# Private buffers for the expert stage, a recurrence in head pairs, a shorter candidate list: one NeuronCore kernel for two transformer blocks

## The chip, the cores and the metric

The kernel is one program on one core of a Trainium2 chip. TensorE (PE) multiplies matrices, VectorE (DVE) and ScalarE (ACT) work on elements, GpSimd (POOL) issues the gathers, SyncE (SP) issues every other transfer. The metric is device time of one execution in microseconds (us): the median of the runs shown.

## The reference

Two blocks follow each other on x of 512 tokens by 1024 columns, all in float32. Cut to what the change touches:

```python
# block 1, four heads of a gated delta rule, 8 chunks of 64 tokens, one after the other
def step(state, inp):
    u_i, w_i, qd_i, kd_i, a_i, gl_i = inp
    v_new = u_i - w_i @ state
    o_i = qd_i @ state + a_i @ v_new
    state = state * gl_i[..., None, None] + jnp.swapaxes(kd_i, -1, -2) @ v_new
    return state, o_i
# beside it, four heads of sparse attention: out = g0 * o_c + g1 * o_s + g2 * o_w
# block 2 ends with product-key experts (8 heads, 128 * 128 experts), 128 tokens at a time
v1, i1 = lax.top_k(s1, 16); v2, i2 = lax.top_k(s2, 16)
cand = (v1[..., :, None] + v2[..., None, :]).reshape(128, 8, -1)      # 256 sums
top_s, pos = lax.top_k(cand, 16)
experts = jnp.take_along_axis(cand_idx, pos, axis=-1)
gate = softmax(top_s)
act = gelu(einsum('chkd,cd->chk', u[experts], hc))
out = einsum('chk,chkd->cd', gate * act, v[experts])
```

## The kernel before

Activations lie transposed, features on the 128 partitions and tokens along the row. A float32 product is made of three fast ones: `split` (lines 192 to 194) writes the high part of a tile by a cast on ACT and the low part by a subtraction on DVE, and `mm3` or `gemm` adds high*high, high*low and low*high in PSUM. The order of instructions on every engine is fixed when the program is built: a list scheduler takes the code in program order as priority and moves work past what waits, as far as buffers allow. So the engines' queues are static, and an instruction that waits holds up all that stands behind it on its engine.

Block 1, the stretch around the change (lines 475 to 484). `proj_qv` makes the projections of one head (three-product GEMMs with 512 columns), `gdn_fin` finishes its chunk matrices, `nsa(t)` does the attention of 128 query tokens for four heads: scores (tiles ks, kw), softmax on DVE and ACT, transposes (L902), products with the values (pt, vn). `gdn_scan` walks the 8 chunks of the recurrence with all four heads side by side: first products w,T (called V here), a subtraction (L753), products w,kN (S), scaling and addition of the state (L759, L760), output products qA,w and at,w (O), a copy (L765). V and O write PSUM bank 0 and S writes bank 1, one tile each, so the next V waits for the copy of this O.

Block 2, `peer`. For 384 of the 512 tokens all 16384 experts are computed densely in 128 blocks of 128 experts, and a gate tensor picks out the selected ones; the last 128 tokens gather the rows of their experts one selected slot at a time. Three parts overlap: `route` finds the 16 best pairs per head and token group (lines 1203 to 1283), `spread` builds the gates by one-hot products (tiles o, L1294 to L1304) and writes them to DRAM, except the last 32 tokens, which stay in glast. Beside both, `run_ahead` does the expert-key GEMM of a block (row, rowhi, rowlo; 24 matmuls) and spills its 128x384 result, 113 to DRAM and 15 kept on chip. The last stage (lines 1120 to 1161) then does for each of the 128 blocks e: load the spilled result (pact) and, for four blocks at once, the gates (gtile); multiply by gtile and by glast (L1139, L1140); split into pwh and pwl; load the expert-value rows into a row buffer and split them into vh and vl; 24 matmuls into eight PSUM banks. `gather_sum` gathers one row of the last 128 tokens' experts per block (L1174, POOL) and adds it into pN on DVE (L1191). Expert-key rows, expert-value rows and these gathered rows share one ring of six row buffers; pact has four buffers, vh, vl, pwh and pwl four.

Of the kernel before, what the change touches and what calls it, by code (L numbers as in the profile page):

```python
# [9 lines left out]
F32 = mybir.dt.float32  # L10
F32R = mybir.dt.float32r
# [4 lines left out]
ALU = mybir.AluOpType  # L16
# [4 lines left out]
P = 128  # L21
S = 512
D = 1024
# [7 lines left out]
ND = 384  # L31
# [119 lines left out]
class Builder:  # L151
# [248 lines left out]
    def block1(self):  # L400
        A, V, x = self.A, self.V, self.x
        with ExitStack() as st1:
# [55 lines left out]
            with ExitStack() as st2:  # L458
                self.gi = self.pool(st2, "gi")
                self.pj = self.pool(st2, "pj")  # L460
                with ExitStack() as nst:
                    self.nk = self.pool(nst, "nk")
                    self.gdn_gates()
                    self.banks(2, 3)
                    for h in range(4):
                        self.proj_k(h, hi, lo, started[h][0] if h < len(started) else None)
                        self.gdn_inv(h)
                    self.banks()
                    self.proj_kv(hi, lo)
                    self.nsa_keys(self.nk)  # L470
                self.mod_queue(0, (2, 4, 3))
                self.proj_nq(hi, lo)
                kp = self.pool(st2, "nt")
                self.nsa_begin(kp)
                for h in range(4):
                    self.proj_qv(h, hi, lo)
                    self.gdn_fin(h)
                    if h < 2:
                        self.nsa(kp, h, False)
                self.gdn_scan()  # L480
                for h in range(4):
                    if h % 2:
                        self.nsa(kp, 2 + h // 2, True)
                    self.proj_gz(h, hi, lo)
            hst.close()
            op = self.pool(st1, "op", side="right")
            mh = self.mh = op.tile([P, KD, S], F32R, name="mh")
# [232 lines left out]
    def gdn_fin(self, h):  # L720
        V, C = self.V, self.C
        r4 = lambda v: v.rearrange("p a b -> p (a b)")
        q, k, vN, E, X = self.qT[h], self.kT[h], self.vN[h], self.at[h], self.X[h]
        psq = self.ps(0)
# [7 lines left out]
        ps = self.ps(0)  # L732
# [5 lines left out]
    def gdn_scan(self):  # L738
        V, C, gi = self.V, self.C, self.gi
        wT, at, qd, kd = self.wT, self.at, self.qd, self.kd  # L740
        St = gi.tile([P, 4, P], F32, name="w0", bufs=2)
        V.memset(St, 0.0)
        oT = self.eq
        for c in range(8):
            t, o = divmod(c * 64, P)
            r = slice(o, o + 64)
            tb = slice(t * P, (t + 1) * P)
            cs = slice(c * 64, c * 64 + 64)
            psv = self.ps(0)
            for h in range(4):  # L750
                self.mm(psv[:, h * P:(h + 1) * P], wT[h][:, tb], St[:, h, :])
            vnew = gi.tile([P, 4, P], F32, name="w1", bufs=2)
            V.tensor_tensor(vnew[r], self.kA[r, :, tb], psv[r].rearrange("p (h d) -> p h d", h=4), ALU.subtract)  # L753
            if c < 7:
                psS = self.ps(1)
                for h in range(4):
                    self.mm(psS[:, h * P:(h + 1) * P], kd[h][r, t, :], vnew[r, h, :])
                Sn = gi.tile([P, 4, P], F32, name="w0", bufs=2)
                V.tensor_tensor(Sn, St, self.gl[:, c, :].unsqueeze(2).to_broadcast([P, 4, P]), ALU.mult)  # L759
                V.tensor_tensor(Sn, Sn, psS.rearrange("p (h d) -> p h d", h=4), ALU.add)  # L760
            pso = self.ps(0)
            for h in range(4):
                self.mm(pso[:, h * P:h * P + 64], St[:, h, :], qd[h][:, cs], True, False)
                self.mm(pso[:, h * P:h * P + 64], vnew[r, h, :], at[h][r, t, o:o + 64], False, True)
            C.copy(oT[:, :, cs], pso.rearrange("p (h b) -> p h b", h=4)[:, :, 0:64])  # L765
            if c < 7:
                St = Sn
        self.oT = oT

    def gdn_out(self):  # L770
        V, C, G, gp, oT = self.V, self.C, self.G, self.gp, self.oT
# [285 lines left out]
    def peer(self):  # L1057
        A, V, C, x = self.A, self.V, self.C, self.x
# [3 lines left out]
        with ExitStack() as st:  # L1062
# [57 lines left out]
            with ExitStack() as st2:  # L1120
                wk = self.pool(st2, "pe")
                bank = [self.ps(m) if m < 6 else self.acc() for m in range(KD)]
                self.sqp = (wk, 4)
                part = []
                for e in range(P):
                    if e == 0 or e % GA == 2:
                        n, e0 = min(GA, P - e) if e else 2, e
                        if e:
                            gt = wk.tile([P, NB - 1, GA, TB], F32, name="gtile", bufs=2)[:, :, :n, :]
                        else:  # L1130
                            gt = self.hN[:, :(NB - 1) * n * TB].rearrange("p (b a t) -> p b a t", b=NB - 1, a=n)
                        self.dma(gt, gd[:, :, e:e + n, :].rearrange("b p a t -> p b a t"))
                    if e < KEPT:
                        act = ra.tile([P, ND], F32, name="pact", bufs=4)
                        self.dma(act, sp[e])
                    else:
                        act = kept[e]
                    a3 = act.rearrange("p (b t) -> p b t", t=TB)
                    V.tensor_tensor(a3[:, :NB - 1, :], a3[:, :NB - 1, :], gt[:, :, e - e0, :], ALU.mult)  # L1139
                    V.tensor_tensor(a3[:, NB - 1, :], a3[:, NB - 1, :], gl[:, e, :], ALU.mult)  # L1140
                    wh = wk.tile([P, ND], F32R, name="pwh", bufs=LAST + 1)
                    wl = wk.tile([P, ND], F32R, name="pwl", bufs=LAST + 1)
                    self.split(wh, wl, act)
# [59 lines left out]
    def route(self, rp, hi, lo, T3, run_ahead):  # L1203
# [7 lines left out]
        self.gi = self.gs_ = 0  # L1211
        qlane = self.lane(rp, "wqr", 2, 2)
        qbank = self.bank_ring(0, 1, acc=0)


        def chosen(px, ix, n, out=None):
# [3 lines left out]
            V.tensor_scalar(ab[:, 0], px, 4, None, ALU.logical_shift_right)  # L1220
            V.tensor_scalar(ab[:, 1], px, 15, None, ALU.bitwise_and)
# [15 lines left out]
        for h in range(8):  # L1237
            first = self.gemms([A["wq"][s] for s in range(2)], hi, lo, lane=qlane, bank=qbank) if h == 0 else None
            for s in range(2):
# [7 lines left out]
                C.copy(sc.rearrange("p a b -> p (a b)"), ps)  # L1247
                for t in (3, 0, 1, 2):
                    self.top16(sc[:, t, :], v_[:, t, h, s, :], ix[:, t, h, s, :])
            for t in (3, 0, 1, 2):  # L1250
                cand = rp.tile([P, 16, 16], F32, name="cand", bufs=2)
                b3 = [P, 16, 16]
                V.tensor_tensor(cand, v_[:, t, h, 0, :].unsqueeze(2).to_broadcast(b3),
                                v_[:, t, h, 1, :].unsqueeze(1).to_broadcast(b3), ALU.add)
                self.top16(cand.rearrange("p a b -> p (a b)"), ts[:, t, h, :], px[:, t, h, :])
# [87 lines left out]
```

## Time and profile before

| | us |
|---|---|
| median of 3 runs | 2481.82 (2474.93 to 2487.04) |
| the profiled execution | 2477.21 |
| its span | 2475.1 |
| PE, DVE, ACT, POOL busy | 2378.9 (96%), 1843.3 (74%), 1077.1 (44%), 337.5 (14%) |

A busy PE is not a PE at its full pace, since records overlap; the pace is the number of matmuls in a stretch (the x behind a busy time). The stages in us from the start of the span: recurrence and attention, 288 to 406; routing with run-ahead GEMMs, 1120 to 1620; gates with run-ahead GEMMs, to 1879; the last stage, to 2458.

### The profile page before, as it was taken

Reading aid. Unit: us, or ns where it says so; the run is one execution under the profiler, and the core shown is the slowest. Engines: PE = TensorE matmul, PEld = TensorE weight load, DVE = VectorE, ACT = ScalarE, POOL = GpSimd, SP = SyncE. Lnnn points to the kernel's source line nnn. Section 1 sums busy time; section 2 is a strip of 40 time slices with the busy share of each in tenths; the row PEclk is TensorE's granted clock in tenths of the full one; section 3 lists DMA queues with packets and bytes.
Section 4 is the critical chain, followed back from the end, with each engine's and each line's share of the span. In section 5 each row is a group of like instructions: output and inputs, shape, how many; then the busy total and the mean of one; then the engine's idle time right before and its main releaser. Section 6 shows DMA issues by size and latency. Waiting matters only on the chain.

```text
span 2475.1 us, 35106 instructions
## 1 busy us (share of the span) xinstructions
PE 2378.9 (96%) x12749; PEld 2150.7 (87%) x12749; DVE 1843.3 (74%) x3826; ACT 1077.1 (44%) x1753; POOL 337.5 (14%) x284
## 2 busy tenths in 40 slices
PE   7999999899999999998999999999998999899998
PEld 7788787678878777877899999999998999899997
DVE  6774635788874389665999999899876777787764
ACT  4534624343332233334323334499995333333332
POOL 0000000000000000000232331233101222223310
PEclk9999989899999999998999999999998999999999
DMA  7341102566554222225478897689867999899981
GB/s 276 125 133 60 52 9 85 170 198 193 188 183 144 81 90 92 70 86 188 148 239 291 319 369 259 202 320 345 321 228 244 301 312 311 301 330 327 325 266 52
DMA packets 197934, 509.40 MB, mean 206 GB/s; under 512 B 20352, under 2 KB 93312, under 8 KB 195840
## 3 DMA queue, kind: packets, MB, share of 16 engines
q1 hardware_dynamic: 160896, 372.92, 44.4%
q0 software_dynamic: 36864, 134.23, 15.3%
q8 instruction: 100, 1.64, 0.3%
q14 instruction: 74, 0.61, 0.1%
HBM read 459.71 MB, written 47.38 MB: 205 GB/s over the span
## 4 chain that ended last, share of the span: by engine, by line
PE 58%; DVE 13%; DMA 13%; issue 7%; ACT 6%; POOL 2%; POOLq 0%; DVEq 0%; SPq 0%; ACTq 0%
PE p L162 38%; PE acc L162 19%; DMA row<-in_ev_dram,eidx 7%; DMA raw<-in_ada_dram 2%; ACT o L1296 1%; POOL row L1174 1%; ACT gstage L1304 1%; DVE grow L1181 1%; DVE pN L1191 1%; DVE wlo L194 1%; DMA araw<-in_ada_dram 1%; DVE vl L194 1%; DMA pact<-spill 1%; ACT rowhi L193 1%; DVE rowlo L194 1%
## 5 line engine op out<-in xcount | busy, mean ns | idle before, releaser
L193 ACT CAST whi<-raw 128x1024 fp32r<-128x1024 f32 (+2 forms) x152 | 150.7, 993 | 386.7 <-PE p L162 239.1
L162 PE MATMUL p<-pwl,vh 128*128 128x384 f32 x768 | 262.7, 342 | 25.0 <-DVE pwl L194 24.5
L162 PE MATMUL p<-pwh,vh 128*128 128x384 f32 x768 | 258.3, 338 | 5.2 <-ACT pwh L193 5.2
L162 PE MATMUL p<-pwh,vl 128*128 128x384 f32 x768 | 259.2, 338 | 0.0
L194 DVE TENSOR_TENSOR wlo<-raw,whi 128x1024 fp32r<-128x1024 f32 (+2 forms) x152 | 174.8, 1151 | 102.9 <-ACT whi L193 100.5
L193 ACT CAST vh<-row 128x1024 fp32r<-128x1024 f32 x128 | 134.3, 1051 | 257.3 <-PE acc L162 186.1
L1174 POOL DMA_INDIRECT row<-in_ev_dram,eidx x128 | 161.1, 1259 | 501.5 <-DVE pN L1191 188.4
L1191 DVE SCALAR_TENSOR_TENSOR pN<-row,dots,pN 128x1024 f32<-128x1024 f32 x127 | 162.7, 1281 | 84.9 <-DMA row<-in_ev_dram,eidx 84.6
L193 ACT CAST rowhi<-row 128x1024 fp32r<-128x1024 f32 x128 | 134.5, 1051 | 206.4 <-PE acc L162 94.6
L194 DVE TENSOR_TENSOR rowlo<-row,rowhi 128x1024 fp32r<-128x1024 f32 x128 | 155.8, 1218 | 35.6 <-ACT rowhi L193 35.5
L162 PE MATMUL p<-hi,rowhi 128*128 128x384 f32 x512 | 174.6, 342 | 3.2 <-ACT hi L301 2.6
L162 PE MATMUL p<-lo,rowhi 128*128 128x384 f32 x512 | 175.5, 343 | 1.8 <-DVE lo L302 1.8
L162 PEld LDWEIGHTS p<-pwl,vh 128*128 128x128 f32 x768 | 146.0, 190 | 35.8 <-DVE pwl L194 35.6
L162 PE MATMUL acc<-lo,rowhi 128*128 128x384 f32 x512 | 175.2, 342 | 0.0
L162 PE MATMUL acc<-hi,rowlo 128*128 128x384 f32 x512 | 174.8, 342 | 0.3 <-DVE rowlo L194 0.3
L162 PE MATMUL acc<-hi,rowhi 128*128 128x384 f32 x512 | 174.5, 341 | 0.6 <-ACT rowhi L193 0.6
L162 PE MATMUL p<-hi,rowlo 128*128 128x384 f32 x512 | 174.9, 342 | 0.1
L194 DVE TENSOR_TENSOR vl<-row,vh 128x1024 fp32r<-128x1024 f32 x128 | 155.9, 1219 | 24.7 <-ACT vh L193 24.7
L162 PE MATMUL p<-hi,whi 128*128 128x512 f32 x416 | 164.8, 402 | 5.7 <-ACT hi L301 4.3
L162 PE MATMUL p<-hi,wlo 128*128 128x512 f32 x416 | 166.8, 401 | 1.1 <-DVE wlo L194 1.0
L162 PE MATMUL p<-lo,whi 128*128 128x512 f32 x416 | 165.6, 399 | 0.9 <-DVE lo L302 0.9
L162 PEld LDWEIGHTS p<-pwh,vh 128*128 128x128 f32 x768 | 145.8, 190 | 5.6 <-ACT pwh L193 5.5
(525 smaller groups left out, 6055.0 us busy)
## 6 DMA issues: line engine op xcount, KB each, us to landing
row<-in_eu_dram SPq DMA_DIRECT2D x128, 512.0 KB
row<-in_ev_dram SPq DMA_DIRECT2D x128, 512.0 KB
araw<-in_ada_dram SPq DMA_DIRECT2D x64, 512.0 KB
raw<-in_up_dram SPq DMA_DIRECT2D x44, 512.0 KB
gdram<-gstage SPq DMA_DIRECT2D x11, 2048.0 KB
gtile<-gdram SPq DMA_DIRECT2D x31, 704.0 KB
spill<-pact SPq DMA_DIRECT2D x113, 192.0 KB
pact<-spill SPq DMA_DIRECT2D x113, 192.0 KB
```

What stands on the lines that cost most here:

```text
L162: self.T.matmul(out, lhsT, rhs, start=start, stop=stop)
L193: self.C.copy(hi, src)
L194: self.V.tensor_tensor(lo, src, hi.bitcast(F32), ALU.subtract)
L1174: self.G.indirect_dma_start(out=u, out_offset=None, in_=self.A[src], in_offset=bass.IndirectOffsetOnAxis(ap=self.eidx[:, s:s + 1], axis=0))
L1181: self.V.scalar_tensor_tensor(u, u, 1.0, self.hN, ALU.mult, ALU.mult, accum_out=self.dots[:, s:s + 1])
L1191: self.V.scalar_tensor_tensor(self.pN, v, w, self.pN, ALU.mult, ALU.add)
L1296: C.activation(o2[:, i, :], self.iota, AF.Abs, bias=T3[:, 1, t:t + 1])
L1304: C.copy(gs[:, :, q * 4:q * 4 + 4].rearrange("p a t -> p t a"), ps.rearrange("p (t a) -> p t a", t=4))
```

## The change

Four edits. (1) The projections run in two head pairs, and the recurrence runs once per pair after its projections; each chunk does two heads, and V, S and O of a chunk share bank 0. The attention of all four token groups stands behind both recurrences, beside the last projections. (2) Of the 256 sums of two sorted lists of 16 only 112 are formed: the first 4 of the one with all 16 of the other, the other 12 with the first 4; `chosen` maps positions in the shorter list back. (3) In the last stage the expert-value rows keep the six row buffers, the gathered rows get six of their own (grow), the spilled results six of their own (vact), and vh, vl use the three high and low pairs of the run-ahead GEMMs and one new pair, in turn. (4) The gates of the last 32 tokens are copied beside the loaded ones on ACT, four blocks at once, so that one multiplication per block does.

```diff
-                for h in range(4):
-                    self.proj_qv(h, hi, lo)
-                    self.gdn_fin(h)
-                    if h < 2:
-                        self.nsa(kp, h, False)
-                self.gdn_scan()
+                for pair in ((0, 1), (2, 3)):
+                    for h in pair:
+                        self.proj_qv(h, hi, lo)
+                        self.gdn_fin(h)
+                    self.gdn_scan(pair)
                 for h in range(4):
-                    if h % 2:
-                        self.nsa(kp, 2 + h // 2, True)
                     self.proj_gz(h, hi, lo)
+                    self.nsa(kp, h, h > 1)
...
+            ps = self.ps(0)
+            psv, psS = half(ps, 0), half(ps, 1)
+            for i, h in enumerate(pair):
+                self.mm(psv[:, i * P:(i + 1) * P], wT[h][:, tb], St[:, i, :])
...
+                pair = lambda: [wk.tile([P, D], F32R, name=n, bufs=1) for n in ("vh", "vl")]
+                vring = ulane[1] * LAST + [pair]
+                self.row = lambda: wk.tile([P, D], F32, name="grow", bufs=6)
...
-                        self.dma(gt, gd[:, :, e:e + n, :].rearrange("b p a t -> p b a t"))
+                        self.dma(gt[:, :NB - 1], gd[:, :, e:e + n, :].rearrange("b p a t -> p b a t"))
+                        C.copy(gt[:, NB - 1], gl[:, e:e + n, :])
                     if e < KEPT:
-                        act = ra.tile([P, ND], F32, name="pact", bufs=4)
+                        act = wk.tile([P, ND], F32, name="vact", bufs=6)
...
-                    V.tensor_tensor(a3[:, :NB - 1, :], a3[:, :NB - 1, :], gt[:, :, e - e0, :], ALU.mult)
-                    V.tensor_tensor(a3[:, NB - 1, :], a3[:, NB - 1, :], gl[:, e, :], ALU.mult)
+                    V.tensor_tensor(a3, a3, gt[:, :, e - e0, :], ALU.mult)
...
-                    vh = wk.tile([P, D], F32R, name="vh", bufs=LAST + 1)
-                    vl = wk.tile([P, D], F32R, name="vl", bufs=LAST + 1)
+                    vring.append(vring.pop(0))
+                    vh, vl = vring[-1]()
...
+            V.tensor_scalar(wide, px, 124, None, ALU.bitwise_and)
+            V.tensor_scalar(wide, wide, 64, 3, ALU.max, ALU.mult)
+            V.scalar_tensor_tensor(wide, wide, 192, px, ALU.subtract, ALU.add)
...
+                for i0, i1, nj in ((0, 4, 16), (4, 16, 4)):
...
+                    V.tensor_tensor(o, a, b, ALU.add)
```

How the queues move, first on PE in the recurrence: a chunk of before, with V (w, T) for four heads, attention products (pc, pt, pr) and S (w, kN).

```order
L878 MATMUL p_2774<-ca,sc 32x128 x4
L162 MATMUL p_2583<-w_2570,T_575 128x128
L162 MATMUL p_2583<-w_2570,T_743 128x128
L162 MATMUL p_2583<-w_2570,T_942 128x128
L162 MATMUL p_2583<-w_2570,T_1141 128x128
L162 MATMUL p_2798<-pc,vcn 128x128
L162 MATMUL p_2798<-pt,vn 128x128 x3
L902 MATMUL p_2811<-ca,pr 128x128 x3
L162 MATMUL p_2838<-pc,vcn 128x128
L162 MATMUL p_2590<-w_2588,kN 128x128 x4
```

The same engine now, at the first of the chunks that stand among attention products:

```order
L162 MATMUL acc<-kw,x 128x384
L162 MATMUL p_2052<-w_2044,T_575 128x128
L162 MATMUL p_2052<-w_2044,T_743 128x128
L162 MATMUL p_2052<-w_2055,kN 128x128 x2
L878 MATMUL p_2494<-ca,sc 32x128 x4
L162 MATMUL p_2052<-qA,w_2044 128x64
L162 MATMUL p_2052<-at,w_2055 128x64
```

A chunk now has two heads, and there are 16. The V of three of them stand among the projection GEMMs, those of thirteen behind them. The stretch behind the projections held 79 GEMM matmuls before and holds 37 now.

Second, ACT at the entry of the last stage, before (glast: the copies of the last gates; vh: the first expert-value rows):

```order
L1296 ACTIVATE o_16285<-ca,T_8309 128x128 x3
L1297 ACTIVATE o_16262<-o_16262 128x384
L1304 COPY glast<-p_16248 128x4x128
L1297 ACTIVATE o_16285<-o_16285 128x384
L1304 COPY glast<-p_16268 128x4x128
L1304 COPY glast<-p_16291 128x4x128
L193 CAST vh<-row 128x1024 x4
L193 CAST pwh<-pact 128x384 x4
```

and now (kept: the result of a run-ahead GEMM; rowhi: here the first three expert-value rows):

```order
L1322 COPY glast<-p_16325 128x4x128
L193 CAST rowhi<-row 128x1024
L1101 ACTIVATE kept_16426<-p_16395 128x384
L1322 COPY glast<-p_16348 128x4x128
L1136 COPY hN<-glast 128x64
L193 CAST rowhi<-row 128x1024
L1101 ACTIVATE kept_16459<-p_16428 128x384
L193 CAST rowhi<-row 128x1024
L1101 ACTIVATE kept_16492<-acc 128x384
L193 CAST rowhi<-row 128x1024
L1101 ACTIVATE kept_16525<-acc 128x384
```

Three run-ahead results are now stored behind the last gate copy, none before; on PE 71 run-ahead matmuls stand behind the last one-hot product, where there were none and the last 20 one-hot products (five rows of four) stood in one run.

Third, DVE in the body of the last stage, two blocks of before and two of now:

```order
L194 TENSOR_TENSOR vl<-row,vh 128x1024
L1139 TENSOR_TENSOR pact<-pact,gtile 128x352
L1140 TENSOR_TENSOR pact<-pact,glast 128x32
L194 TENSOR_TENSOR pwl<-pact,pwh 128x384
L1191 SCALAR_TENSOR_TENSOR pN<-row,dots,pN 128x1024
```

```order
L194 TENSOR_TENSOR rowlo<-row,rowhi 128x1024
L194 TENSOR_TENSOR pwl<-vact,pwh 128x384
L1143 TENSOR_TENSOR vact<-vact,gtile 128x384
L1194 SCALAR_TENSOR_TENSOR pN<-grow,dots,pN 128x1024
L194 TENSOR_TENSOR vl<-row,vh 128x1024
```

The sum into pN keeps its place in the queue; the row that it reads now comes from its own ring.

## Rows read from the trace of the kernel before

**Rows 1.** Windows: busy us (instructions) of PE, PEld, DVE, ACT, POOL; PE clock; DMA share; GB/s.
```profile
288.00:406.00 118.00, 114.32 (x581) 90.36 (x580) 49.56 (x137) 39.62 (x98) 0.00 (x0) 0.84 0.06 20
...
1310.00:1560.00 250.00, 248.78 (x1422) 248.07 (x1421) 244.47 (x621) 94.89 (x132) 65.34 (x60) 1.00 0.84 302
...
1869.00:1894.00 25.00, 15.81 (x72) 14.63 (x72) 14.51 (x45) 16.01 (x28) 5.47 (x3) 0.73 0.68 211
1894.00:2160.00 266.00, 249.27 (x1391) 241.68 (x1390) 193.49 (x287) 88.55 (x117) 61.79 (x56) 0.99 0.88 301
2180.00:2260.00 80.00, 80.00 (x464) 80.00 (x463) 63.25 (x95) 28.51 (x38) 23.64 (x19) 1.00 0.94 331
2260.00:2400.00 140.00, 132.71 (x753) 129.93 (x752) 107.73 (x162) 47.49 (x63) 42.74 (x25) 1.00 0.91 311
```
**Rows 2.** Waits in the last stage, 1894 to 2400: us in total, times, longest.
```profile
POOL row L1174 <- DVE vl L194: 157.8, 42, 9.3
...
DVE pN L1191 <- DMA row<-in_ev_dram,eidx: 76.1, 50, 5.7
DVE pact L1139 <- DMA pact<-spill: 48.3, 39, 2.9
...
PE p L162 <- DVE pwl L194: 23.6, 24, 2.4
```
**Rows 3.** Instruction groups, 1894 to 2400: busy us, mean ns, idle before them.
```profile
L194 DVE TENSOR_TENSOR vl<-row,vh 128x1024 fp32r<-128x1024 f32 x113 | 137.7, 1218 | 0.0
L1191 DVE SCALAR_TENSOR_TENSOR pN<-row,dots,pN 128x1024 f32<-128x1024 f32 x106 | 135.9, 1282 | 76.3 <-DMA row<-in_ev_dram,eidx 76.1
...
L194 DVE TENSOR_TENSOR pwl<-pact,pwh 128x384 fp32r<-128x384 f32 x109 | 60.1, 551 | 0.0
L1139 DVE TENSOR_TENSOR pact<-pact,gtile 128x352 f32<-128x352 f32 x109 | 56.9, 522 | 48.5 <-DMA pact<-spill 48.3
...
L1140 DVE TENSOR_TENSOR pact<-pact,glast 128x32 f32<-128x32 f32 x109 | 20.3, 186 | 0.0
```
**Rows 4.** Issues of transfers, 1900 to 2400: kind, count, KB each.
```profile
row<-in_ev_dram SPq DMA_DIRECT2D x113, 512.0 KB
pact<-spill SPq DMA_DIRECT2D x105, 192.0 KB
gtile<-gdram SPq DMA_DIRECT2D x28, 704.0 KB
```
**Rows 5.** PE at the entry of the last stage: start, us, work [idle before].
```profile
1869.17 1.95 PE L162 MATMUL p<-o,o 128*128 128x128 f32 x16
...
1883.87 2.29 PE L162 MATMUL p<-pwh,vh 128*128 128x384 f32 x6 [5.19 <-ACT pwh L193]
...
1888.55 0.52 PE L162 MATMUL p<-pwl,vh 128*128 128x384 f32 x1
1888.87 0.52 PE L162 MATMUL p<-pwh,vl 128*128 128x384 f32 x1
```
**Rows 6.** ACT there.
```profile
1879.53 3.88 ACT L193 CAST vh<-row 128x1024 fp32r<-128x1024 f32 x4
```
**Rows 7.** PE groups of the recurrence, 288 to 406.
```profile
L162 PE MATMUL p<-at,w 64*128 64x64 f32 x64 | 15.7, 330 | 0.0
L162 PE MATMUL p<-qA,w 128*128 128x64 f32 x64 | 15.3, 324 | 0.1
...
L162 PE MATMUL p<-w,T 128*128 128x128 f32 x64 | 10.3, 314 | 0.0
...
L162 PE MATMUL p<-w,kN 64*128 64x128 f32 x56 | 9.0, 307 | 0.8 <-DVE w L753 0.8
```
**Rows 8.** One window inside that stretch, columns as in rows 1.
```profile
320.00:340.00 20.00, 20.00 (x80) 16.60 (x80) 3.67 (x9) 4.24 (x11) 0.00 (x0) 0.57 0.00 1
```
**Rows 9.** DVE groups of the routing, 1180 to 1545.
```profile
L1198 DVE MATCH_REPLACE8 rsc<-tv,rsc 128x128 f32<-128x128 f32 x56 | 15.6, 289 | 0.0
...
L1198 DVE MATCH_REPLACE8 cand<-ts,cand 128x256 f32<-128x256 f32 x32 | 13.2, 413 | 0.0
```

More of the change, by code (lines that the diff above doesn't have):

```diff
@@ L723, in gdn_fin @@
         q, k, vN, E, X = self.qT[h], self.kT[h], self.vN[h], self.at[h], self.X[h]
-        psq = self.ps(0)
+        psq = self.ps(4)
         for t in range(TT):
@@ L731, in gdn_fin @@
         V.tensor_tensor(vN, vN, self.rn[:, h, :].unsqueeze(2).to_broadcast([P, TT, P]), ALU.mult)
-        ps = self.ps(0)
+        ps = self.ps(4)
         for t in range(TT):
@@ L735, in gdn_fin, with gdn_scan @@
         C.copy(k, ps)
-    def gdn_scan(self):
+    def gdn_scan(self, pair):
         V, C, gi = self.V, self.C, self.gi
         wT, at, qd, kd = self.wT, self.at, self.qd, self.kd
-        St = gi.tile([P, 4, P], F32, name="w0", bufs=2)
+        h0 = pair[0]
+        hs = slice(h0, h0 + 2)
+        new = lambda k: gi.tile([P, 4, P], F32, name=f"w{k}", bufs=2)[:, 0:2, :]
+        St = new(0)
         V.memset(St, 0.0)
-        oT = self.eq
+        oT = self.oT = self.eq
+        half = lambda ps, i: ps[:, i * 2 * P:(i + 1) * 2 * P]
         for c in range(8):
@@ L748, in gdn_scan @@
             cs = slice(c * 64, c * 64 + 64)
[L749 to L753, printed above, removed]
-            if c < 7:
[L755 to L765, printed above, removed]
+            ps = self.ps(0)
+            psv, psS = half(ps, 0), half(ps, 1)
+            for i, h in enumerate(pair):
+                self.mm(psv[:, i * P:(i + 1) * P], wT[h][:, tb], St[:, i, :])
+            vnew = new(1)
+            V.tensor_tensor(vnew[r], self.kA[r, hs, tb], psv[r].rearrange("p (h d) -> p h d", h=2), ALU.subtract)
+            if c < 7:
+                for i, h in enumerate(pair):
+                    self.mm(psS[:, i * P:(i + 1) * P], kd[h][r, t, :], vnew[r, i, :])
+                Sn = new(0)
+                V.tensor_tensor(Sn, St, self.gl[:, c, hs].unsqueeze(2).to_broadcast([P, 2, P]), ALU.mult)
+                V.tensor_tensor(Sn, Sn, psS.rearrange("p (h d) -> p h d", h=2), ALU.add)
+            for i, h in enumerate(pair):
+                self.mm(psv[:, i * P:i * P + 64], St[:, i, :], qd[h][:, cs], True, False)
+                self.mm(psv[:, i * P:i * P + 64], vnew[r, i, :], at[h][r, t, o:o + 64], False, True)
+            C.copy(oT[:, hs, cs], psv.rearrange("p (h b) -> p h b", h=2)[:, :, 0:64])
             if c < 7:
                 St = Sn
-        self.oT = oT
     def gdn_out(self):
@@ L1128, in peer @@
                         if e:
-                            gt = wk.tile([P, NB - 1, GA, TB], F32, name="gtile", bufs=2)[:, :, :n, :]
+                            gt = wk.tile([P, NB, GA, TB], F32, name="gtile", bufs=2)[:, :, :n, :]
                         else:
-                            gt = self.hN[:, :(NB - 1) * n * TB].rearrange("p (b a t) -> p b a t", b=NB - 1, a=n)
-                        self.dma(gt, gd[:, :, e:e + n, :].rearrange("b p a t -> p b a t"))
+                            gt = self.hN[:, :NB * n * TB].rearrange("p (b a t) -> p b a t", b=NB, a=n)
+                        self.dma(gt[:, :NB - 1], gd[:, :, e:e + n, :].rearrange("b p a t -> p b a t"))
+                        C.copy(gt[:, NB - 1], gl[:, e:e + n, :])
                     if e < KEPT:
-                        act = ra.tile([P, ND], F32, name="pact", bufs=4)
+                        act = wk.tile([P, ND], F32, name="vact", bufs=6)
                         self.dma(act, sp[e])
@@ L1213, in route @@
         qbank = self.bank_ring(0, 1, acc=0)
+        NC = 112
         def chosen(px, ix, n, out=None):
@@ L1219, in chosen @@
             ab = rp.tile([P, 2, n, 16], U32, name=f"ab{n}", bufs=1)
[L1220 to L1221 removed]
+            wide = ab[:, 0]
+            V.tensor_scalar(wide, px, 124, None, ALU.bitwise_and)
+            V.tensor_scalar(wide, wide, 64, 3, ALU.max, ALU.mult)
+            V.scalar_tensor_tensor(wide, wide, 192, px, ALU.subtract, ALU.add)
+            V.tensor_scalar(ab[:, 1], wide, 15, None, ALU.bitwise_and)
+            V.tensor_scalar(wide, wide, 4, None, ALU.logical_shift_right)
             abf = rp.tile([P, 2, n, 16], F32, name=f"abf{n}", bufs=1)
@@ L1249, in route @@
                     self.top16(sc[:, t, :], v_[:, t, h, s, :], ix[:, t, h, s, :])
-            for t in (3, 0, 1, 2):
[L1251 to L1255, printed above, removed]
+            cands = {}
+            for t0, n in ((3, 1), (0, 3)):
+                cand = rp.tile([P, n, NC], F32, name=f"cand{n}", bufs=1)
+                for i0, i1, nj in ((0, 4, 16), (4, 16, 4)):
+                    b4 = [P, n, i1 - i0, nj]
+                    o = cand[:, :, 0:64] if i0 == 0 else cand[:, :, 64:NC]
+                    o = o.rearrange("p t (i j) -> p t i j", j=nj)
+                    a = v_[:, t0:t0 + n, h, 0, i0:i1].unsqueeze(3).to_broadcast(b4)
+                    b = v_[:, t0:t0 + n, h, 1, 0:nj].unsqueeze(2).to_broadcast(b4)
+                    if n == 1:
+                        o, a, b = (v.squeeze(1) if hasattr(v, "squeeze") else v[:, 0] for v in (o, a, b))
+                    V.tensor_tensor(o, a, b, ALU.add)
+                cands.update({t0 + i: cand[:, i, :] for i in range(n)})
+            for t in (3, 0, 1, 2):
+                self.top16(cands[t], ts[:, t, h, :], px[:, t, h, :])
                 if t == 3:
```

## The prediction

> **What bounds the kernel now.** I read the windows by stage first, because PE is busy almost everywhere and only the number of matmuls tells whether it runs at its pace. In the last stage the window 2180 to 2260 holds 464 matmuls in 80 us, 5.80 per us, with the clock at 1.00 throughout [rows 1]; that is the pace when nothing is late. From 1894 to 2160 there are 1391 where 266 * 5.80 = 1543 would fit: 152 / 5.80 = 26 us are missing. From 2260 to 2400 it is 753 of 812: 10 us. The body of the stage thus loses 36 us. The entry, 1869 to 1894, holds 72 matmuls in 25 us: 40 one-hot products at 1.95 / 16 = 0.12 us and 32 others at 0.17, some 10.4 us of work, so 14.6 us are lost; 5.19 of them are one wait for pwh, and after it matmuls stand 0.32 us apart (1888.55, 1888.87) instead of 0.17, with the granted clock at 0.73 in the window, between its two levels of 1.2 and 2.4 GHz [rows 1, 5].
>
> The waits then say why. PE waits for pwl from DVE (23.6 us in 24 cases), and DVE was late because it had stood 76.1 us before the sum into pN for a gathered row and 48.3 us for a spilled result [rows 2]. The gather was late because POOL had waited 157.8 us for DVE to free a row buffer of the shared ring by a vl [rows 2]. So the last stage is short of buffers, not of an engine: DVE's work per block is 1.218 + 1.282 + 0.551 + 0.522 + 0.186 = 3.76 us [rows 3] against 24 / 5.80 = 4.14 us of PE.
>
> In the routing, 1310 to 1560, DVE is busy for 244.47 of 250 us and PE for 248.78 at clock 1.00 [rows 1]: DVE looks like the bound, but PE is filled by run-ahead GEMMs. Around the recurrence, 288 to 406, the clock is 0.84 on average, worth 0.16 * 118 = 19 us, while PE counts as busy for 114.32 us [rows 1].
>
> **The change part by part.** *Buffers, body of the last stage.* Removed is the dependence of a gather on a vl and of an expert-value load on a pN. With six buffers a gather can be issued some six blocks, 25 us, before its sum; the longest wait for one was 5.7 us [rows 2]. Six vact instead of four does the same for the spilled results. The depth of vh, vl stays at four pairs. What is late next is the transfers themselves: a block needs 512 KB of values, 512 of gathered rows, 192 of results and 704 / 4 of gates [rows 4], a gathered tile having the shape of a value tile, 1392 KB or 1.425 MB per 4.14 us, that is 344 GB/s. The window at full pace moved 331 GB/s at a share of 0.94, 352 at a full one [rows 1]. That is enough, with 2% to spare. So I do not give back all 36 us: 27 are gained, 9 stay. Ends: 0, if the transfers cannot run closer than they do (they could even lose a few us, since vact lies in memory that the gates stage uses and cannot be filled ahead as pact was), and 36.
>
> *One gate multiplication.* DVE saves 186 ns per block and pays for 32 columns more, (522 - 186) / 320 * 32 = 34 ns: 0.15 us of 3.76 [rows 3]. DVE then has 0.5 us per block in hand; PE hides it, so it counts nothing by itself. ACT gets one copy of 128x128 per four blocks, and it is busy for 88.55 of 266 us [rows 1]. Nothing.
>
> *Entry.* The scheduler now leaves 71 run-ahead matmuls behind the last one-hot product, 71 / 5.80 = 12.2 us of PE work over the time in which the gates' memory comes free. But the chain to the first new matmul hangs on the end of these: value rows 0 to 2 use the run-ahead pairs, so the cast of the third waits for the last GEMM; DVE has five low parts in its queue ahead of the first gate multiplication; and on SP the first vact load stands behind eight value rows, of which the eighth waits for the low part of the second. After the last GEMM come a cast (3.88 / 4 = 0.97) [rows 6], a low part (1.22), a multiplication (0.56), a cast of pwh (0.97 * 384 / 1024 = 0.4): 3.2 us, say 5 with the load among many in flight. The clock will fall as it did after the 5.19 us, when some 24 matmuls stood at 0.32 instead of 0.17: 3.5 us. Lost 8.5 instead of 14.6: 6 us gained. Ends: 0 (as now) and 14.
>
> *Recurrence and attention.* The matmuls stay the same. The four groups of the recurrence hold PE for 15.7 + 15.3 + 10.3 + 9.0 = 50.3 us [rows 7], 3.1 per half chunk. Moved from the sparse stretch to the projections are 42 GEMM matmuls (0.17 * 512 / 384 = 0.23 each, 9.7 us) and 3 of 16 half chunks (9 us); moved into it is the attention of the first two token groups, some 8 us. The sparse stretch shrinks to about 108 us and the stretch of 226 to 288 grows by the same 10: PE's sum is unchanged, and what can change is waits and clock. For it: the recurrence has priority over the attention, chunks of two heads are short, and the projections get fillers. Against it: V and S of a chunk stand next to each other on PE in places, with the subtraction between them and nothing to fill; V, S and O wait in one bank; thirteen chunks in a row instead of eight; and fewer GEMMs beside them. I take 0, at the clock 0.84 of now. Ends: 22 us gained (19 of clock, 3 of waits), and 51 lost if all of the 108 us went at the 0.57 that the window 320 to 340 shows [rows 8]: 108 * 0.84 / 0.57 = 159.
>
> *112 sums.* From 128 to 256 columns a pass takes 413 - 289 = 124 ns more [rows 9], so 112 instead of 256 saves 0.14 us, five passes for 32 candidate lists: 22 us of DVE; the sums save some 4 more, the mapping of positions costs about as much. PE hides all of it: in 1310 to 1560 it was busy for all but 1.2 us [rows 1]. What appears is an earlier start of the gates, which leaves the run-ahead GEMMs for the entry (counted there). 2 us gained; ends -2 and 5.
>
> Sum: 27 + 6 + 0 + 2 = 35 us off the profiled execution's 2477.2 (span 2475.1 and 2.1 around it): 2442. The median of the runs is 4.6 higher than that execution, within their spread; I keep 2442.
>
> **Rivals.** *The transfers bind (R1).* The stage moved 301 GB/s at 0.88 while it waited [rows 1]: for it, that the need of 344 is nearly what a full share gives; against it, that 80 us went at full pace. If the body keeps 30 of 36 us and the first blocks wait 3 us longer for vact, the gain is 6 + 3 + 2 = 11: 2466. The Trainium skill, DMA: Bandwidth & Descriptors, section Queues, rings and completion order, says that an engine takes turns between its queues packet by packet. By that rule six gathers queued ahead would slow the SP queue's loads; by it the time would be R1's. No row here shows both queues full, so it speaks for R1 and moves it up a little.
>
> *Slower (R2).* The sparse stretch of block 1 falls to the low clock for all of its length: 51 us lost, 35 gained elsewhere, 2493. It decides once the stretch's granted clock is below about 0.58, where the loss passes 47. For it: the window 320 to 340, where the clock did stay at 0.57 with PE never idle [rows 8]; against it, that it came back and the stretch's mean is 0.84 [rows 1]. The Trainium skill, Perfetto Trace Analysis, section Matmul Optimizations, holds that matmuls should run back to back in batches, since their engine's power follows its use; by that rule this edit goes the wrong way and R2 and R3 are likelier.
>
> *Half of that (R3).* The stretch loses 20 us by waits between V and S and some clock, the last stage gains as forecast: 2462.
>
> *Both well (R4).* The stretch gains the 22 us: 2420.
>
> **How the numbers follow.** Forecast 0.52 (2430 to 2456), R4 0.12, R3 0.14, R1 0.16, R2 0.06. A measurement of this kernel can tell about 0.5% from no change, 12 us: faster means below 2469. R3 is mostly so (0.10), R1 about half (0.07): 0.52 + 0.12 + 0.10 + 0.07 = 0.81 faster; slower 0.06 (R2); the rest, 0.13, the same. The range is 2412 to 2472: R2, half of R1's upper side and the far end of R4 are left out.
>
> **What would show it.** Right: in the last stage 5.7 to 5.8 matmuls per us from entry to 2400, waits of DVE for gathered rows under 15 us, POOL no longer waiting for vl; a DMA share of 0.94 or more. One PE wait of 3 to 6 us between the last run-ahead matmul and the first pwh. DVE's share in the routing lower by some 20 us with PE as full as before. Block 1 as long to within 20 us up to 425. Wrong: a body still at 5.2 matmuls per us (R1), or a granted clock under 0.7 in the attention stretch (R2, R3).

## The result, and the profile after

The changed kernel takes 2447.26 us (median; 2434.46 to 2453.95), before 2481.34 on the same chip: ratio 0.9857, interval 0.981 to 0.9904. The forecast was 2442. In a later comparison the same kernel took 2444.74 against 2487.24: 0.9833 (0.9803 to 0.9862). The profiled execution is the fastest of its four, 2434.46 us with a span of 2432.7; this matters below.

Windows of the changed kernel, columns as in [rows 1]:

```profile
288.00:406.00 118.00, 113.91 (x648) 90.21 (x647) 67.76 (x224) 53.59 (x139) 3.45 (x1) 0.94 0.11 37
1310.00:1560.00 250.00, 250.00 (x1429) 249.69 (x1428) 235.33 (x563) 103.33 (x153) 79.72 (x55) 1.00 0.81 293
1560.00:1620.00 60.00, 56.31 (x337) 55.05 (x336) 36.72 (x81) 39.28 (x77) 14.72 (x13) 0.97 0.68 220
...
1880.00:1894.00 14.00, 14.00 (x68) 14.00 (x68) 10.45 (x15) 4.09 (x8) 6.21 (x6) 0.81 1.04 379
1894.00:2160.00 266.00, 265.97 (x1535) 265.65 (x1534) 219.32 (x263) 99.47 (x144) 89.51 (x68) 1.00 1.01 363
...
2160.00:2400.00 240.00, 240.00 (x1387) 240.00 (x1386) 173.25 (x215) 89.71 (x129) 34.69 (x35) 1.00 0.78 267
```

From 1894 to 2160 PE does 1535 matmuls, 5.77 per us, where before had 1391 [rows 1]; from 2160 to 2400 it is 1387, 5.78. DMA works at a share of 1.01 up to 2160 and of 0.78 behind it. In the routing PE is as full as before, and DVE has 9 us more to spare from 1310 to 1560; from 1120 to 1614 its busy time falls from 456.1 to 435.3 us, the some 20 that the prediction named. But from 1560 to 1620 PE, full in before (60.00 of 60 us, 345 matmuls), now stands idle for 3.7 us, with the clock at 0.97.

Waits of the changed kernel in the last stage, 1894 to 2400 (us in total, times, longest):

```profile
POOL grow L1177 <- DVE pN L1194: 284.0, 101, 10.5
...
DVE vact L1143 <- DMA vact<-spill: 8.4, 2, 7.6
```

POOL waits for the sums now, no longer for vl, and that costs nothing. The 76.1 us that DVE stood for gathered rows and the 23.6 that PE stood for pwl [rows 2] are gone from the list. The next two lists are the gates: first the changed kernel, 1554 to 1863, then before, 1614 to 1879.

```profile
DVE row L1184 <- DMA row<-in_er_dram,eidx: 32.8, 10, 6.0
...
PE p L162 <- DVE o L1320: 14.4, 7, 4.9
DVE pN L1194 <- DMA row<-in_ev_dram,eidx: 13.6, 6, 4.9
```

```profile
DVE pN L1191 <- DMA row<-in_ev_dram,eidx: 8.5, 5, 2.0
...
DVE row L1181 <- DMA row<-in_er_dram,eidx: 3.1, 3, 2.4
```

DVE stands 46 us for gathered rows there instead of 12. One such wait in the changed kernel, on DVE and then on PE:

```profile
1640.18 1.22 DVE L194 TENSOR_TENSOR rowlo<-row,rowhi 128x1024 fp32r<-128x1024 f32 x1
1646.94 1.23 DVE L1184 SCALAR_TENSOR_TENSOR row<-row,hN 128x1024 f32<-128x1024 f32 x1 [5.55 <-DMA row<-in_er_dram,eidx]
...
1649.23 0.86 DVE L1320 TENSOR_SCALAR o<-ca,T 128x128 f32<-128x128 f32 x3
```

```profile
1649.72 2.69 PE L162 MATMUL p<-o,o 128*128 128x128 f32 x11 [4.95 <-DVE o L1320]
```

The one-hot tables stand in DVE's queue behind the product with the gathered row, and PE has a one-hot product at the head of its own. The entry, on PE:

```profile
1874.89 0.34 PE L162 MATMUL acc<-hi,rowlo 128*128 128x384 f32 x1
1879.62 2.29 PE L162 MATMUL p<-pwh,rowhi 128*128 128x384 f32 x6 [4.39 <-ACT pwh L193]
1881.71 0.52 PE L162 MATMUL acc<-pwh,rowhi 128*128 128x384 f32 x1
```

Run-ahead GEMMs fill PE up to 1875, then comes one wait of 4.39 us, as against 5.19 [rows 5] with idle places ahead of it.

To sum this up by stage I compare profiled executions at equal PE work: matmuls in their order, each counted with its pitch at the full clock (0.174 us for 384 columns). The marks are 500, 1450, 1700, 1750 and 2250 us of such work, which before reached at 603, 1589, 1847, 1913 and 2448 us. Entries are us gained on before's profiled execution; names are those of the experiments below. The columns are cut by work, so their names are rough: the column of the gates takes in the last 30 us of before's routing.

```
                to 603  routing  gates  entry  last stage   sum
changed          15.6     0.5   -18.4    8.8     36.0      42.5
e8_after          0.8    -2.3   -18.1    8.9     36.3      25.6
e1_last           0.8    -0.9    -3.1   -4.2     36.3      28.9
e2_scan           0.0    -0.9    -5.0    1.6    -15.8     -20.1
e3_sums          -2.4    -2.4   -17.5   11.5     36.3      25.5
e4_nosums         2.8    -2.2    -4.5   -5.1     36.2      27.2
e5_behind        -4.5     0.3     0.1    2.5     36.3      34.7
e6_dots           2.7    -3.5   -16.0    5.2     36.3      24.7
e7_dots256        7.5    -3.1   -30.7   -8.1     36.2       1.8
e9_split          3.8   -17.1    -2.7   11.8     36.3      32.1
e10_after_split  11.0   -20.1    -2.6    9.7     29.2      27.2
e11_swap          2.9    -2.5    -4.8   11.6     36.3      43.5
e12_after_swap    3.0     0.0    -4.8    9.2     24.3      31.7
```

Before's profiled execution (2477) was some 9 us faster than its median on the chips of the experiments (2486), so a sum of 27 here is a difference of medians of some 36, give or take where a run's own profiled execution stands among its others (e2_scan's is 12 us slower than its median).

### The profile page after: what moved, and what is told of

It is laid out like the page before. It is cut to its first block, busy times and chain, and to the rows that moved or that the text cites. A ratio compares the mean times of both kernels' runs of the same rounds, so it can differ in the third digit from the quotient of the medians.

```text
span 2432.7 us, 34959 instructions
## 1 busy us (share of the span) xinstructions
PE 2355.3 (97%) x12749; PEld 2144.3 (88%) x12749; DVE 1812.3 (74%) x3754; ACT 1075.5 (44%) x1788; POOL 339.5 (14%) x284
## 4 chain that ended last, share of the span: by engine, by line
PE 81%; DVE 8%; DMA 7%; ACT 2%; issue 2%; POOL 0%; SPq 0%; POOLq 0%; DVEq 0%; ACTq 0%
PE p L162 54%; PE acc L162 26%; DMA row<-in_er_dram,eidx 2%; DMA araw<-in_ada_dram 1%; DMA raw<-in_ada_dram 1%; DMA row<-in_ev_dram,eidx 1%; DVE rowlo L194 1%; DVE raw L335 1%; DVE grow L1184 1%; DVE wlo L194 1%; ACT whi L193 1%; PE p L902 0%; DVE araw L335 0%; DVE tix L1203 0%; DVE ny L300 0%
## 5 line engine op out<-in xcount | busy, mean ns | idle before, releaser
L194 DVE TENSOR_TENSOR rowlo<-row,rowhi 128x1024 fp32r<-128x1024 f32 x224 | 272.9, 1219 | 133.3 <-ACT rowhi L193 129.3
L162 PE MATMUL p<-pwh,rowhi 128*128 128x384 f32 x576 | 193.0, 337 | 4.4 <-ACT pwh L193 4.4
L162 PE MATMUL p<-pwl,rowhi 128*128 128x384 f32 x576 | 193.4, 336 | 0.0
L162 PE MATMUL p<-pwh,rowlo 128*128 128x384 f32 x576 | 193.3, 336 | 0.0
L1177 POOL DMA_INDIRECT grow<-in_ev_dram,eidx x112 | 133.6, 1193 | 355.8 <-DVE pN L1194 289.1
L1177 POOL DMA_INDIRECT grow<-in_er_dram,eidx x91 | 124.1, 1364 | 240.3 <-DVE tix L1200 101.4
L1194 DVE SCALAR_TENSOR_TENSOR pN<-grow,dots,pN 128x1024 f32<-128x1024 f32 x112 | 143.1, 1278 | 3.0 <-DMA grow<-in_ev_dram,eidx 3.0
L162 PE MATMUL acc<-hi,whi 128*128 128x512 f32 x352 | 142.3, 405 | 0.0
L162 PE MATMUL acc<-lo,whi 128*128 128x512 f32 x352 | 141.6, 402 | 0.0
L162 PE MATMUL acc<-hi,wlo 128*128 128x512 f32 x352 | 140.7, 400 | 0.0
```

The source lines that it names most:

```text
L162: self.T.matmul(out, lhsT, rhs, start=start, stop=stop)
L194: self.V.tensor_tensor(lo, src, hi.bitcast(F32), ALU.subtract)
L1177: self.G.indirect_dma_start(out=u, out_offset=None, in_=self.A[src], in_offset=bass.IndirectOffsetOnAxis(ap=self.eidx[:, s:s + 1], axis=0))
L1194: self.V.scalar_tensor_tensor(self.pN, v, w, self.pN, ALU.mult, ALU.add)
```

## The experiments

Each ratio is to before on the same chip.

**The parts alone.** e1_last is before with the last stage's lines of the change, e2_scan with those of block 1 (which also move two products of `gdn_fin` to another PSUM bank), e3_sums with those of the routing, e4_nosums the change without the routing's.

```diff
 e1_last, e4_nosums
+                self.row = lambda: wk.tile([P, D], F32, name="grow", bufs=6)
+                        act = wk.tile([P, ND], F32, name="vact", bufs=6)
...
 e2_scan, e4_nosums
+                for pair in ((0, 1), (2, 3)):
...
+                    self.gdn_scan(pair)
...
 e3_sums
+        NC = 112
...
+                self.top16(cands[t], ts[:, t, h, :], px[:, t, h, :])
```

e1_last. 

> Before with the last stage's edit alone (own gather buffers, vact, one gate multiplication). Own-part theory (each stage of the two profiles gains by its own edit, the parts add): the body of the last stage loses nothing any more, 36 us gained, 5.75 matmuls per us or more from 1900 to 2400; the entry is as before, because no GEMM matmuls are left over for it; the gates stage as before: ratio 0.985. Rival A (the entry's 9 us also come from these buffers): 45 us, 0.982. Rival B (the body was helped by the earlier edits too): under 25 us, 0.990 or more.

Measured 0.984 (0.9818 to 0.9863), 36.3 us in the last stage: the own-part theory. The ratio alone would allow rival A too, but the entry gains nothing, it even loses 4.2.

e2_scan. 

> Before with the recurrence by head pairs and all attention behind it, alone. Own-part theory: 15 us gained up to the end of block 1, with the granted clock of 288 to 406 at 0.92 or more, nothing afterwards: ratio 0.994. Rival (the clock of that stretch differs from execution to execution whatever the order): 0.998 to 1.002, and a clock of 0.84 to 0.9 in the profile.

Measured 0.9981 (0.9956 to 1.0005): the rival, with a clock from 288 to 406 of 0.83, a little below its range; the interval leaves room for a gain of a few us. Its profiled execution was the slowest of its twelve (2469.61 to 2497.12), and DVE stood 103.5 us for gathered rows in the last stage.

e3_sums. 

> Before with the 112 sums alone. Own-part theory: the gates start earlier, all of the last 37 gathered rows fall into them, DVE stands for them for some 30 us with the one-hot tables queued behind, PE loses 18 us in the gates stage; the entry gets back 9 by the GEMM matmuls left over: 9 us slower, ratio 1.004. Rival A (the waits in the gates of the changed kernel were chance or belong to another edit): no loss there, 9 us faster, 0.996. Rival B (the 22 us that DVE saves do count): 0.991.

Measured 0.9843 (0.982 to 0.9867), below all three forecasts. The gates lost 17.5 and the entry won 11.5, as the first theory said. What none had foreseen: the last stage, not a line of which was touched, also gained the full 36.3. Its waits on DVE there, 1894 to 2400, with the shared ring of six:

```profile
DVE vl L194 <- ACT vh L193: 54.9, 56, 2.5
DVE pN L1191 <- DMA row<-in_ev_dram,eidx: 13.0, 8, 3.3
```

e4_nosums. 

> The changed kernel with 256 sums as before. Own-part theory: the 18 us of the gates stage come back and the 9 us of the entry go; 15 + 36 = 51 us faster than before, ratio 0.979, and 9 us faster than the changed kernel. Rival A (gates' waits were chance): 0.986 to 0.989, no faster than the changed kernel.

Measured 0.9832 (0.9809 to 0.9854), not told apart from the changed kernel. The gates' loss is nearly gone (4.5) as the first theory said, but the entry loses 5.1 where the changed kernel wins 8.8: gates and entry together cost 9.6 us without the short lists and 9.2 to 9.6 with them. Nor do the 15 us of block 1 come back (2.8). The parts do not add: the buffers and the short lists each bring the 36 us alone, and they can be had once.

**Why the 112 sums cure the last stage.** e3_sums has before's buffers, so their number cannot be the reason, and I looked at how the six are used. In before a gathered row is read soon after its issue. POOL, DVE and SP of before:

```profile
2008.85 1.01 POOL L1174 DMA_INDIRECT row<-in_ev_dram,eidx  x1 [4.31 <-DVE vl L194]
```

```profile
2010.69 1.22 DVE L194 TENSOR_TENSOR vl<-row,vh 128x1024 fp32r<-128x1024 f32 x1
...
2015.66 1.28 DVE L1191 SCALAR_TENSOR_TENSOR pN<-row,dots,pN 128x1024 f32<-128x1024 f32 x1
```

```profile
1992.95 0.33 SPq L1145 DMA_DIRECT2D row<-in_ev_dram  x1
```

The row gathered at 2008.85 is summed from 2015.66 on; the value row that vl reads at 2010.69 was issued at 1992.95. Over 1900 to 2300, from the issue times and the ends of the readers (which transfer goes into which buffer is taken from the compiled program), a gathered row holds its buffer for 8.3 us and a value row for 18.6; in e3_sums it is 11.4 and 13.1. Two rows per block share six buffers, so at full pace the two have 6 * 4.14 = 24.8 us together; before's 26.9 is a slower turn with DVE standing in it. The order of DVE's instructions shows the cause: in before the sum runs one to two blocks ahead of the value row beside which its buffer is handed out, in e3_sums beside it or just behind. Why the scheduler fell into one or the other is not shown; what was still queued at the entry differs between the two.

e5_behind puts the sum back into its place and leaves the rest of the code as in before (the scheduler orders all of it anew, so a few sums more are left for the last stage):

```diff
+                    if self.gs_ < P:
+                        w = self.dots[:, self.gs_:self.gs_ + 1]
+                        V.scalar_tensor_tensor(w, vl[:, 0:1].bitcast(F32), 0.0, w, ALU.mult, ALU.add)
                     self.gather_sum(1)
```

> Before, with one tiny DVE operation per block (one column of vl times 0 added to the weight of the block's sum), which holds the sum of a gathered row behind the low part of the value row beside which its buffer is given out; in before it ran two blocks ahead of it. Buffers, gate multiplications and the routing are those of before. Balance theory (the ring of six is not too small, it is badly shared: a value row holds a buffer for 19 us and a gathered row for 8, and DVE waits for the latter): both hold theirs for 11 to 14 us, DVE's wait for gathered rows falls from 76 to under 30 us, the last stage runs at 5.7 matmuls per us or more from 1900 on, 30 us gained: ratio 0.987. Rival (too few buffers, as the prediction had it): the waits stay, and the added operations cost a little: 1.000 to 1.005.

Measured 0.9836 (0.9821 to 0.9851). Windows, then DVE's waits, 1894 to 2400:

```profile
1894.00:2160.00 266.00, 266.00 (x1537) 266.00 (x1536) 230.66 (x390) 93.64 (x128) 72.47 (x65) 1.00 0.99 349
2160.00:2360.00 200.00, 200.00 (x1156) 200.00 (x1155) 172.18 (x286) 70.67 (x96) 40.82 (x42) 1.00 0.97 337
```

```profile
DVE vl L194 <- ACT vh L193: 51.4, 60, 2.5
...
DVE pN L1194 <- DMA row<-in_ev_dram,eidx: 1.0, 2, 0.5
```

A gathered row now holds its buffer for 12.1 us and a value row for 12.4, the sum stands one block behind that value row (blocks 20 to 99), PE waits for nothing in this stretch, and the whole gain of the change is there with before's buffers. The balance theory holds; the gain is 6 us more than it said. Runs also scatter less: 2443.86 to 2449.39, before on that chip 2481.39 to 2492.26.

**What the gates lose.** e6_dots moves products from the gates into the routing; e7_dots256 does it with 256 sums; e8_after is the changed kernel again.

```diff
-                self.gather_dot((1 + i % 2) * (h > 0))
+                self.gather_dot((2 - (i in (2, 6))) * (h > 0))
```

e6_dots. 

> The changed kernel with 16 instead of 13 products with gathered rows per head in the routing, so that 16 instead of 37 are left for the gates. Gates theory (the 18 us that PE loses there come from DVE standing for gathered rows with one-hot tables queued behind): the loss falls to 8 us or less, and the routing stays full on PE since its DVE work goes up by 21 * 1.22 = 26 us, what the sums had freed: 10 us faster than the changed kernel, ratio 0.979 to 0.981. Rival (the loss belongs to the earlier start itself, not to the gathers): PE's loss in the gates stays at 15 to 18 us, 0.984 or more.

Measured 0.9852 (0.9828 to 0.9875): no gain. The waits went from the products to the sums (gates, 1615 to 1887):

```profile
DVE pN L1194 <- DMA row<-in_ev_dram,eidx: 27.6, 11, 7.5
DVE row L1184 <- DMA row<-in_er_dram,eidx: 4.3, 3, 2.9
```

The loss stayed at 16.0, as the rival said. But the gates started at 1615, as late as in before (1614), so the earlier start is not the reason either. Holding times (issue to the end of the reading, issues from the first gate table to the last one-hot product) point to the ring once more: a row of a run-ahead GEMM holds a buffer for 21 us in before, for 26 in the changed kernel, for 34 here, and a gathered value row for 11, 10 and 8.

e7_dots256. 

> The same 16 products per head, with the 256 sums of before (else the changed kernel). If DVE is at its limit in the routing of before, as its 244 of 250 busy us say, the 26 us more show there: PE loses 10 to 25 us in the routing, ratio 0.987 to 0.993. If PE hides them all: as e4_nosums or up to 4 us faster, 0.981 to 0.983.

Measured 0.9943 (0.9923 to 0.9964), a little above the first range. PE loses some 20 us where the routing ends, between 1600 and 1645, with 144 matmuls where 45 * 5.75 = 259 would fit:

```profile
1600.00:1645.00 45.00, 32.44 (x144) 29.56 (x142) 40.60 (x48) 9.27 (x17) 20.71 (x12) 0.81 0.82 276
```

The rest of the 30.7 in the table falls into the gates, where DVE stands 28.3 us for gathered value rows (1645 to 1913). DVE cannot take 26 us more in the routing with the long lists (115 products made by 1600, 94 in before); with the short ones it can (e6_dots: 114). The gap between the two medians, 22.7 us, is about the DVE time that the 112 sums free: real, but hidden as long as nothing uses it. That the two sizes agree may be chance, since the gap lies in the gates (14.7) and the entry (13.3).

e8_after. 

> The changed kernel again, for a second profile. If the 15 us that its first profile gained in block 1 came from the clock of that execution, this one gains 0 to 6 us there, its clock from 288 to 406 is 0.80 to 0.90 and its time some 2447; if they come from the order, 12 us or more are gained again. The 18 us lost in the gates and the 9 won at the entry are there again.

Measured above. Gates -18.1, entry 8.9, last stage 36.3: repeated. Block 1: 0.8 instead of 15.6, by this row:

```profile
288.00:406.00 118.00, 113.91 (x570) 90.16 (x569) 57.58 (x193) 48.36 (x125) 0.00 (x0) 0.83 0.05 18
```

The same program had 0.94 in its first profile: all but 0.8 of the 15.6 us belong to that execution. A gain of a few us by the order is neither shown nor excluded: up to 603 the eight profiles with the new order gained 0.0 to 15.6 us, 5.4 in the mean, and the other five with the old one -4.5 to 3.8, 0.1 in the mean.

**Parting the ring.** e9_split is e3_sums with the operation of e5_behind and this; e10_after_split makes the same edits in the changed kernel.

```diff
-            ulane = self.lane(gw, "row", 6, 3)
+            ulane = self.lane(gw, "row", 3, 3)
...
-            self.row = ulane[0]
+            self.row = lambda: gw.tile([P, D], F32, name="grow", bufs=3)
```

e9_split. 

> Before with the 112 sums, the small operation of e5_behind, and the ring of six parted from the gates on: three buffers for the rows of the run-ahead GEMMs and the expert values, three for gathered rows. In the gates of the changed kernel a GEMM row holds a buffer for 24 us and a gathered one for 10, and DVE stands 45 to 48 us for gathered rows. Balance theory for the gates: DVE's wait there falls to 20 us or less, PE loses 6 us or less instead of 17, the entry keeps its 9 us and the last stage its full pace: 10 us faster than the 112 sums alone, ratio 0.979 to 0.981. Rival (three rows are too few for the GEMMs): PE waits for rowhi in the routing or the gates, 10 us or more, 0.985 or more.

Measured 0.9843 (0.9811 to 0.9876): no faster than e3_sums. DVE stood 0.4 us for gathered rows in the gates and PE lost 2.7 there, but the routing lost 17.1, most of it here:

```profile
1460.00:1480.00 20.00, 17.80 (x100) 17.04 (x99) 19.83 (x50) 8.00 (x11) 14.92 (x11) 1.00 1.03 414
1480.00:1500.00 20.00, 15.07 (x73) 14.39 (x72) 20.00 (x28) 8.25 (x11) 3.56 (x3) 0.83 0.73 261
```

Neither half is a clean test. With three buffers of their own, the products that e3_sums leaves for the gates ran ahead into the routing: all 128 were made before the first gate table, 91 in e3_sums. So the gates had only sums left to wait for. And in the routing DVE was full (59.83 of 60 us from 1440 to 1500): by 1500 it had made 98 products, 88 in e3_sums, 10 * 1.22 = 12 us more of work. PE waited there for low parts from DVE (4.4 us) and for casts from ACT (2.7), which waited for rows. Whether three rows or the added products cost the 17.1 us is not shown.

e10_after_split. 

> The changed kernel with the same parting of the ring in the gates (three and three) and the same small operation; its six own gather buffers of the last stage are replaced by these three, vact and the one gate multiplication stay. Balance theory: as e9_split, 0.978 to 0.981, the last stage at 5.75 matmuls per us with 3 + 3 buffers instead of 6 + 6. Rival: 0.985 or more, by PE waits for rowhi, or by waits for value rows in the last stage, which would show that the number of buffers counts there after all.

Measured 0.9892 (0.9855 to 0.9929), in the rival's range. The expectation misdescribes the kernel in one point: the six own gather buffers stayed, and it is the value rows that have three. Gates and routing went as in e9_split, with all 128 products ahead of the gates here too; the last stage gained 29.2 of 36.

e11_swap and e12_after_swap keep six buffers for the GEMMs' rows until the routing ends:

```diff
+            rst = ExitStack()
+            rows = [self.pool(rst, "r6"), 6]
+            ulane = (lambda: rows[0].tile([P, 1024], F32, name="row", bufs=rows[1]), ulane[1])
...
+            rst.close()
+            rows[:] = [self.pool(st, "r3"), 3]
+            self.row = lambda: rows[0].tile([P, D], F32, name="grow", bufs=3)
```

e11_swap. 

> As e9_split, but six row buffers for the GEMMs until the routing ends, and three and three only from the gates on (the memory is given back and handed out anew). e9_split lost 11 us between 1440 and 1500, where three rows came too late, and 3 in the gates, DVE standing 0.4 us there for gathered rows. If both readings hold, the 11 us come back and the gates stay as there: 10 us faster than e9_split, ratio 0.979 to 0.981. Rival: the handing over makes GEMM rows wait once at the end of the routing, 8 us or more: 0.983 or more.

Measured 2436.18 us (2433.62 to 2439.61), 0.9808 (0.9784 to 0.9832): the fastest of all, below the changed kernel's median by 8 to 11 us, though the intervals of the ratios overlap a little with those of the changed kernel. Here the small ring does not exist before the gates, so only 91 products stand ahead of the first table, as in e3_sums: this is the test of the balance theory that e9_split was not. The routing lost 2.5 and the gates 4.8 instead of 17.5, although they started at 1570, and the entry won 11.6. First DVE's wait for gathered rows in the gates (1570 to 1854; 30.2 and 18.2 us in e3_sums), then the window in which e9_split lost most:

```profile
DVE grow L1189 <- DMA grow<-in_er_dram,eidx: 3.5, 2, 2.1
```

```profile
1440.00:1500.00 60.00, 60.00 (x342) 60.00 (x342) 55.95 (x137) 25.98 (x34) 20.36 (x16) 1.00 0.89 326
```

A GEMM row issued in the gates holds its buffer for 20 us (26 in e3_sums). So the gates' loss came from the shared ring.

e12_after_swap. 

> The changed kernel with the same handing over and the small operation of e5_behind (its own six gather buffers in the last stage stay, value rows have three there). As e11_swap, 0.978 to 0.981, if three value rows do in the last stage; if its start waits for value rows as in e10_after_split (5 us), 0.983.

Measured 0.9828 (0.9801 to 0.9855): routing and gates as forecast, but 12 us missing in the first blocks of the last stage, where PE waited 6.7 us for pwh and 3.2 for rowhi, both from ACT, the entry's own wait of 3.5 among them. ACT in turn stood 11.6 us for two value rows (1870 to 1960), the longest 8.5 us, and the changed kernel shows no such wait: the expectation's second branch. e11_swap too has three value rows there and loses nothing, so their number alone is not the reason; which of the other lines of the last stage it is stays open.

## Why the prediction was right

The total is 5 us off, the sum under it less good: three of its terms erred (+9, +3, -20), and that the errors nearly cancel is luck. The main mechanism held, DVE's waits for gathered rows in the last stage; its reason did not, nor did the four edits each bring their part: e1_last, e3_sums and e5_behind alone (0.984, 0.9843, 0.9836) are not told apart from the whole change.

- *Body of the last stage.* Forecast 27 of 36 us, measured 36.0 and 36.3; of the loss nothing stays. That the waits of DVE for gathered rows set the pace was right. "So the last stage is short of buffers, not of an engine" was not: e5_behind has no more buffers and loses nothing. Private buffers cured the stage all the same, since they end the sharing. The coupling by the ring was seen; how unevenly its two users held it was not asked. POOL's 157.8 us behind vl [rows 2] held the answer: a gathered row had to wait for a buffer that a value row had kept for long.
- *One gate multiplication.* It takes 550 ns (forecast 556). e5_behind, with two multiplications, reaches the same pace, so it counted nothing, as forecast.
- *Entry.* Forecast 6, measured 8.8 and 8.9, with the wait of 3 to 6 us measured as 4.39 and slow matmuls behind it (clock 0.81 from 1880 to 1894). It comes from the GEMMs left over by the 112 sums (11.5 in e3_sums), not from the buffers (-4.2 in e1_last).
- *Recurrence and attention.* Forecast 0; e2_scan 0.0 up to 603 and a ratio that spans 1. No gain by the order is shown; the clock moves by execution, and the changed kernel's first profile happened to be a fast one.
- *112 sums.* This step failed. "PE hides all of it" holds up to 1589 (0.5 and -2.3). "What appears is an earlier start of the gates, which leaves the run-ahead GEMMs for the entry" left out what else then falls into the gates: before had made 98 of the 128 products when the first table of the gates was due, the changed kernel 91, and the remaining gathers stand in one ring with GEMM rows that hold it longer (e11_swap parts the ring and loses 4.8). Forecast +2 with an end of -2; measured -18. With the entry's share the short lists are worth nothing here: gates and entry cost 9.2 to 9.6 us with them, 9.6 without (e4_nosums). On lists of 112 a pass takes 255 to 264 ns against 413 [rows 9], a little less than sized (413 - 140 = 273).
- *Rivals.* The transfers did not bind (R1): the body ran at full pace with a share of 1.01 and 363 GB/s, more than the 352 that I took for a full share. The turn-taking of queues that the Trainium skill describes (DMA: Bandwidth & Descriptors, section Queues, rings and completion order) may be at work, but the full pace shows no cost of it here. R2 and R3 did not happen: the stretch from 288 to 406 had clocks of 0.83 to 0.94 in the eight profiles with the new order, and of 0.75 to 0.86 in the six with the old one. R4's 22 us were 15.6 in one execution and 0.8 in the next.

## What to carry to other kernels

When a ring of buffers has two users, compare how long each holds one, from the issue to the end of the reading: if one of them holds twice as long as the other and the other's reader stands, the order (here in the last stage, e5_behind) or a parting of the ring (here in the gates, e11_swap) can cure it, and more buffers are only one way. A parted ring also lets its user run ahead into the stage before, so look where that work lands (e9_split). When a step off the critical path is made faster, ask which waits it had kept apart from the next stage. And profile a kernel twice before a stage's gain is put down to an edit.

## What was not expected of the hardware

The last stage ran from 1894 to 2160 at a DMA share of 1.01 to 1.02 and 361 to 366 GB/s (e1_last, e8_after) with PE at 5.65 matmuls per us or more, and 20 us of e9_split (1460 to 1480) at 414, with PE at 5.0 there. In one program the granted clock of the same stretch was 0.94 in one execution and 0.83 in the next, worth 15 us.
